# Score runs that wait for their banks' readers, with the rest of each run at the highest priority

## The chip, the core and the metric

The kernel runs on one core of a Trainium2 chip, in one launch. The metric is the device time in microseconds of one execution. The engines named below are TensorE (PE; its weight loads are shown as PEld), VectorE (DVE), ScalarE (ACT), GpSimd (POOL) and SyncE (SP), which issues nearly all DMAs.

## What is computed

One layer of a hybrid backbone for 128 context tokens and 512 latent tokens (a grid of 8 x 64), with width 1024. The core of the reference:

```python
def _trunk_layer(x, mod, ...):
    shift, scale, gate = jnp.split(mod, 3, axis=-1)
    h = _rmsnorm(x, g_pre) * (1 + scale) + shift
    proj = h @ w_in
    qa, ka, va, ga, qr, zf, zb, ir, gr, uf, gf = _split_columns(proj)
    ...
    oa = _context_attention(qa, ka, va)            # context tokens
    oa = _neighbourhood_attention(qa, ka, va, ctx_kv[0], ctx_kv[1], rpb)   # latent tokens
    o_r, s_fin = _hgrn_bidir(qr, zf, zb, ir, lb_f, lb_b, s0)
    o_f = _fourier(uf, w_fnet)
    mixed = jnp.concatenate([oa * silu(ga), o_r * silu(gr), o_f * silu(gf)], axis=-1)
    out = mixed @ w_out
    x = x + gate * _rmsnorm(out, g_post)
```

The attention has 8 heads of 64. A latent token reads keys of its neighbourhood and 256 cached context keys in one softmax; a context token reads the 128 context keys.

## The kernel before

All 640 tokens are normalised, modulated and kept transposed as `hT`, split in a high and a low part so that three products of the short float format make one precise product. Each block of 128 columns of the input projection is 2 x 24 products of 128x320 (`block`), from a weight load `raw` that ACT and DVE split in `hi` and `lo`. Blocks feed the three branches: attention in four pairs of heads (`attention_blocks`, `attention`), the recurrence in two (`recurrence`), the Fourier mixing (`fourier_blocks`, `fourier`), and the gates. At the end `out_first` and `out_second` make the output projection.

The order in which the program is written comes from `Order`: generators run as streams by estimated times. That order gives every instruction its priority; a scheduler, which simulates the engines, then picks on each engine the ready instruction that stands first. So the order on PE is the scheduler's. Afterwards each engine runs its own list strictly in that order, and semaphores hold an instruction until what it needs is done.

A pair of heads in `attention(p)` has five units: `softmax_latent(0..3)`, each for 128 latent tokens, then `softmax_context` (written as unit 4). A latent unit's scores are two calls of `scores`, six products each, which alternate between the two heads (`hh` 1 and 0): head 1 lies in partitions 64 to 127, head 0 in 0 to 63, so that neighbours use different halves of the array. Each head's products go to a bank of its own. `follow` ties each product behind the one before it on PE, but lets others come between. The softmax is a maximum (L675), the addition of the bias table with a maximum (L676), a negation (L678), two exponentials (L679, L680), a sum, a reciprocal and a scaling (L681 to L683) per head. Then `transposes` makes four 128x128 transposes per head into one bank (L124), and `split` brings them out: a cast on ACT (L127) and a subtraction on DVE (L128), two of each. A unit's transposes are written after the scores of the unit behind it (`AHEAD = 2`). `weighted` multiplies with the values.

The banks: eight, of which five rotate for most tiles (`pb` tag "b", the scores and transposes among them) and three for the blocks of the input projection and some others (tag "f"). A tile that gets a bank again waits for the last readers of that bank. There are two buffers `pe` for the exponentials, one for each head.

`mod_cols` makes the modulation: eight products (two instructions each) with 32 columns, on four column strips, for a weight tile.

Of the kernel before, what the change touches and what calls it, by code (L numbers as in the profile page):

```python
# [9 lines left out]
F32 = mybir.dt.float32  # L10
F32R = mybir.dt.float32r
U32 = mybir.dt.uint32
ACT = mybir.ActivationFunctionType
# [4 lines left out]
P = 128  # L18
# [53 lines left out]
def mixer_kernel(ctx: ExitStack, tc: tile.TileContext, A, O):  # L72
    nc = tc.nc
    sc, ve, gp, te, sy = nc.scalar, nc.vector, nc.gpsimd, nc.tensor, nc.sync
# [35 lines left out]
    def mm(out, lhsT, rhs, start=True, stop=True):  # L110
        n, m = rhs.free_size(), lhsT.free_size()
        od.now += 1e-3 * (n * 0.4167 * 4 if rhs.dtype == F32 else max(n * 0.4167, m * 0.83)) + 2e-3
        return te.matmul(out, lhsT, rhs, start=start, stop=stop).ins  # L113

    def follow(chain, ins):

        if chain:
            tc.add_manual_dep(ins, chain[-1].name, mybir.DependencyInfo(mybir.DependencyClass.NoSync,
                                                                        mybir.DependencyReason.DATA), reason="turns")
        chain.append(ins)  # L120
# [4 lines left out]

    def split(src, hi, lo, hi_eng=None, lo_eng=None):
        (sc.copy if hi_eng is None else hi_eng.tensor_copy)(hi, src)  # L127
        (ve if lo_eng is None else lo_eng).tensor_sub(lo, src, hi.bitcast(F32))  # L128


    ident = cp.tile([P, P], F32, tag="ident", name="ident")
# [2 lines left out]
    def const(name, shape, dt=F32, dma=gp.dma_start):  # L134
        t = cp.tile([P, *shape], dt, tag=name, name=name)
        if name in A:
            dma(t, A[name])
        return t
# [6 lines left out]
    RS = [slice(0, 64), slice(64, 128)]  # L145
# [20 lines left out]
    csil = const("csil", [KT, 32])  # L166
# [22 lines left out]
        with tc.issue_after(wdma[-1]) if wdma else ExitStack():  # L189
            sy.dma_start(t, src)  # L190

    def mod_cols(out, w):

        t = od.now
        for k in range(KT):
            o = out[32 * (k % 4):32 * (k % 4) + 32, :]
            mm(o, csil[:, k, :], w[:, k, :], start=(k < 4), stop=(k >= 4))
        od.now = t + 0.45

    shift, G, rstd = const("shift", [KT, 2]), const("G", [KT, 2]), const("rstd", [5])  # L200
# [14 lines left out]
    def load_x():  # L215
        for i in range(5):
            load(xa[i], A["x"][i * P:(i + 1) * P, 0:NT])
            load(xb[i], A["x"][i * P:(i + 1) * P, NT:D])
# [23 lines left out]
    def start_stream():  # L242
        load_x()
        raws, zraw = [], []

        def loads(k):
            for u in range(2):
                raws.append(load_raw(A["wss"][2 * k + u], RAW[2 * k + u]))
            if k < 2:
                zraw.append(load_raw(A["win"][k], "raw"))  # L250

        for k in range(EARLY):
            loads(k)
        scale_x()
        od.now = 11.0
        for k in range(KT):
            if k + EARLY < KT:
                loads(k + EARLY)
            row = sp.tile([P, 256], F32, tag="AC", name=nm("row"), bufs=2)
            pm = PB()  # L260
            for u in range(2):
                mod_cols(pm[:, u * P:(u + 1) * P], raws[2 * k + u])
            yield 0
            ve.tensor_copy(row, pm[:, 0:256])
            yield LAT["row"]

            for u in range(2):
                tr(pm[:, u * P:(u + 1) * P], row[:, u * P:(u + 1) * P])
            pt = S(4)
            ve.reduce_sum(pt, pm[:, 0:256].rearrange("p (u g r) -> p u r g", u=2, r=32)[:, :, 0:2, :], axis=AX.X)  # L270
            ve.tensor_scalar(G[:, k, :], pt[:, 0:2], bss[:, k, 0:1], 1.0, op0=ALU.add, op1=ALU.add)
            ve.tensor_scalar_mul(G[:, k, :], G[:, k, :], gpre[:, k:k + 1])  # L272
            ve.tensor_scalar_add(shift[:, k, :], pt[:, 2:4], bss[:, k, 1:2])
            modulated(k, pm)
            if k < 2:
                zf_w.append(split_w(zraw[k]))
            if k == 1:
                od.set("zw", 0.0)
            yield max(0.0, 13.5 + 2.7 * (k + 1) - od.now)
# [134 lines left out]
    def recurrence(p):  # L414
# [16 lines left out]
        def level(KB, QB, li):  # L431


            mk = late["masks"][:, li, :].unsqueeze(1)
            for i0, i1 in ((0, 4), (4, 5)):
                pa = [PB(), PB()]
                t, chain = od.now, []
                for i in range(i0, i1):
                    for hh in (1, 0):
                        ins = mm(pa[hh][:, (i - i0) * P:(i - i0 + 1) * P], KB[RS[hh], i * P:(i + 1) * P],  # L440
                                 QB[RS[hh], i * P:(i + 1) * P])
                        follow(chain, ins)
                od.now = 0.5 * (t + od.now)
                for hh in range(2):
                    out = AL[:, hh] if i0 == 0 else AC[:, hh:hh + 1, :]
                    src = pa[hh][:, :(i1 - i0) * P].rearrange("p (a t) -> p a t", t=P)
                    if li == 0:
                        sc.copy(out, src)
                    else:
                        ve.copy_predicated(out, mk.to_broadcast([P, i1 - i0, P]), src)  # L450

        for li, h in enumerate(LEVELS):
            QB, KB = T(), T()
# [76 lines left out]
        for i in range(5):  # L530
            o = po[i // 4][:, i % 4 * P:i % 4 * P + P]
# [5 lines left out]
        os_, sq, ss = T(), T(), S(10)  # L537
# [31 lines left out]


    att = [None] * 4

    def attention_blocks(p):
        tbl = sp.tile([P, 2, 2, 256], F32, tag="tbl", name=nm("tbl"), bufs=WB["tbl"])
# [62 lines left out]
    def attention(p):  # L637
        yield f"a{p}"
        tbl, qs, ks, kcs, vs = att[p]

        def scores(outs, qt, keys, chain):

            cols, t = slice(qt * P, (qt + 1) * P), od.now
            for n, (a, b) in enumerate(((0, 0), (0, 1), (1, 0))):
                for hh in (1, 0):
                    follow(chain, mm(outs[hh], qs[a][RS[hh], cols], keys(b)[RS[hh]], start=(n == 0), stop=(n == 2)))
            od.now = 0.5 * (t + od.now)

        os_ = tp.tile([P, NT], F32, tag="o", name=nm("o"), bufs=WB["o"])

        def softmax_context():
            pss, pes = [PB(), PB()], []
            scores([t[:, 0:P] for t in pss], 0, lambda b: ks[b][:, 0:P], [])
            for hh in range(2):
                m, pe = S(4), PE_()
                ve.reduce_max(m[:, 0:1], pss[hh][:, 0:P], axis=AX.X)
                ve.tensor_scalar_mul(m[:, 1:2], m[:, 0:1], -1.0)
                sc.activation(pe[:, 0:P], pss[hh][:, 0:P], ACT.Exp, bias=m[:, 1:2], accum_out=m[:, 2:3])
                ve.reciprocal(m[:, 2:3], m[:, 2:3])
                NE.tensor_scalar(pe[:, :P], pe[:, :P], m[:, 2:3], 0.5, op0=ALU.mult, op1=ALU.mult)  # L660
                pes.append(pe)
            return pes
# [5 lines left out]

        def softmax_latent(qt):
            pss, pes, chain = [PB(), PB()], [], []  # L670
            scores([t[:, 256:512] for t in pss], 1 + qt, lambda b: kcs[b], chain)
            scores([t[:, 0:256] for t in pss], 1 + qt, lambda b: latent_keys(b, qt), chain)
            for hh in range(2):
                m, pe, sb, ss = S(4), PE_(), S(256), pss[hh]
                ve.reduce_max(m[:, 0:1], ss[:, 256:512], axis=AX.X)  # L675
                ve.tensor_tensor_reduce(sb, ss[:, 0:256], tbl[:, int(qt == 3), hh, :], 1.0, m[:, 0:1],  # L676
                                        op0=ALU.add, op1=ALU.max, accum_out=m[:, 1:2])
                ve.tensor_scalar_mul(m[:, 1:2], m[:, 1:2], -1.0)  # L678
                sc.activation(pe[:, 256:512], ss[:, 256:512], ACT.Exp, bias=m[:, 1:2], accum_out=m[:, 3:4])  # L679
                sc.activation(pe[:, 0:256], sb, ACT.Exp, bias=m[:, 1:2], accum_out=m[:, 2:3])  # L680
                ve.tensor_add(m[:, 2:3], m[:, 2:3], m[:, 3:4])  # L681
                ve.reciprocal(m[:, 2:3], m[:, 2:3])
                NE.tensor_scalar(pe, pe, m[:, 2:3], 0.5, op0=ALU.mult, op1=ALU.mult)  # L683
                pes.append(pe)
            return pes
# [19 lines left out]
        def transposes(qt, pe, pT):  # L705
            ptr = PB()
            for g in range(4):

                gd = 1 - g if (qt == 1 and g < 2) else g
                tr(ptr[:, gd * P:(gd + 1) * P], pe[:, g * P:(g + 1) * P])  # L710
            for b in range(2):
                split(ptr[:, b * 256:b * 256 + 256].rearrange("p (g t) -> p g t", t=P),
                      pT[b][0][:, :, qt, :], pT[b][1][:, :, qt, :])

        def weighted(hh, pT):
            r, o = RS[hh], RS[1 - hh]
# [127 lines left out]
    def gate_vectors():  # L844
        selr = cp.tile([P, 2, P], F32R, tag="selr", name="selr")
        gp.tensor_copy(selr, sel)
        for q in range(8):
            yield f"block{WG + q}"
            hf = q // 4
            w = load_raw(A["wg"][q], "raw")  # L850
# [10 lines left out]
            if q % 2 == 0:  # L861
                rows = [sp.tile([P, 256], F32R, tag="AC", name=nm("row"), bufs=2) for _ in range(2)]
            pm, es = PB("f"), slice(q % 2 * P, q % 2 * P + P)
            mod_cols(pm[:, 0:P], w)
            split(pm[:, 0:P], *[t[:, es] for t in rows])
            if q % 2 == 0:
                continue
# [5 lines left out]
            for d in range(2):  # L873
                g = gg[d][hf][:, cs]
# [254 lines left out]
```

## Time and profile before

| | |
|---|---|
| time, median of 3 runs | 437.03 us (436.5 to 437.03) |
| the profiled execution | 437.11 us, span 435.3 us |
| PE busy | 411.3 us (94%) |
| DVE busy | 303.5 us (70%) |
| ACT busy | 205.8 us (47%) |
| DMA | 47.62 MB, mean 109 GB/s |

The span goes from the first instruction to the last; the time has some 1.8 us around it. A row of a timeline has its start and length in us, the engine, the line of the kernel, the operation, out<-in by the program's names, the shape and the count; in brackets stands the idle time before it and what ended it. Lengths of PE's products are modelled and overlap: the pace is read from one start to the next.

### The profile page before, as it was taken

The numbers are of one execution on the slowest core, as the hardware profiler recorded it, in microseconds if no ns is written. First come the engines' busy times: TensorE is split into PE (matmuls) and PEld (weight loads), VectorE is DVE, ScalarE is ACT, GpSimd is POOL, SyncE is SP. The second block draws the span as 40 slices with busy tenths as digits, with TensorE's granted clock in tenths as the row PEclk, the third lists the DMA queues.
The fourth block names the chain that finished last, engine by engine and source line by source line (L and its number), as shares of the span: only waits on it lengthen the run. The fifth ranks groups of instructions, "written<-read, shape, count | busy, mean of one in ns | idle before, by whom it ended". The sixth has DMA issues, their size and how long they took to land.

```text
span 435.3 us, 8309 instructions
## 1 busy us (share of the span) xinstructions
PE 411.3 (94%) x3176; PEld 372.7 (86%) x3176; DVE 303.5 (70%) x866; ACT 205.8 (47%) x546; POOL 7.4 (2%) x23
## 2 busy tenths in 40 slices
PE   0699999999998999999999999999999999999994
PEld 0488899999988998999899889889898988988884
DVE  2775479999986866885597658885768928670174
ACT  6434467565341526654444444753556643350161
POOL 2000000000020100000000000000000000000000
PEclk9999999999999999999999999999999999999998
DMA  7996153211302021122021413245134302481023
GB/s 236 412 407 229 49 158 114 74 45 50 88 20 76 10 62 48 56 97 74 32 68 60 145 50 104 98 147 163 51 119 150 96 0 66 140 291 48 0 105 139
DMA packets 19528, 47.62 MB, mean 109 GB/s; under 512 B 3184, under 2 KB 6912, under 8 KB 19488
## 3 DMA queue, kind: packets, MB, share of 16 engines
q1 hardware_dynamic: 19376, 46.94, 32.0%
q8 instruction: 25, 0.41, 0.4%
q0 software_dynamic: 112, 0.14, 0.3%
q14 instruction: 15, 0.12, 0.1%
HBM read 43.80 MB, written 3.28 MB: 108 GB/s over the span
## 4 chain that ended last, share of the span: by engine, by line
PE 90%; DVE 3%; DMA 3%; ACT 1%; issue 1%; SPq 0%; DVEq 0%; ACTq 0%
PE pb L113 84%; PE pb L124 7%; DMA vs<-wss 2%; DMA txa<-x 1%; DVE AL L450 1%; DVE t L524 1%; DVE AL L487 0%; ACT L679 0%; DVE t L951 0%; ACT pe L680 0%; DVE t L467 0%; DVE t L466 0%; DVE AC L450 0%; DVE t L468 0%; SPq L190 0%
## 5 line engine op out<-in xcount | busy, mean ns | idle before, releaser
L113 PE MATMUL pb<-hT,hi 128*128 128x320 f32 x896 | 208.7, 317 | 2.5 <-DVE vs L128 1.5
L113 PEld LDWEIGHTS pb<-hT,hi 128*128 128x128 f32 x896 | 148.7, 188 | 9.0 <-issue 3.3
L113 PE MATMUL pb<-hT,lo 128*128 128x320 f32 x448 | 139.1, 312 | 0.0
L113 PEld LDWEIGHTS pb<-hT,lo 128*128 128x128 f32 x448 | 84.0, 188 | 1.3 <-DVE G L272 0.2
L128 DVE TENSOR_TENSOR lo<-raw,hi 128x1024 fp32r<-128x1024 f32 x35 | 42.8, 1223 | 18.7 <-ACT hi L127 18.5
L127 ACT CAST hi<-raw 128x1024 fp32r<-128x1024 f32 x35 | 36.8, 1050 | 28.4 <-PE pb L113 17.5
L113 PE MATMUL pb<-t,t 64*128 64x128 f32 (+2 forms) x414 | 42.9, 291 | 0.4 <-DVE AL L450 0.4
L113 PEld LDWEIGHTS pb<-t,t 64*128 64x128 f32 (+1 forms) x414 | 36.0, 188 | 4.7 <-issue 0.7
L127 ACT CAST pT<-pb 128x256 fp32r<-128x256 f32 x64 | 23.5, 373 | 22.3 <-DVE pT L128 11.1
L113 PE MATMUL pb<-hi,mh 128*128 128x512 f32 (+1 forms) x108 | 30.8, 375 | 0.0
L128 DVE TENSOR_TENSOR pT<-pb,pT 128x256 fp32r<-128x256 f32 x64 | 26.5, 419 | 1.7 <-ACT pT L127 1.5
L679 ACT ACTIVATE pe<-pb,s 128x256 f32<-128x256 f32 x32 | 15.3, 478 | 17.5 <-DVE s L678 8.4
L113 PEld LDWEIGHTS pb<-hi,mh 128*128 128x128 f32 x108 | 19.6, 188 | 3.7 <-DVE mh L128 0.3
L113 PE MATMUL pb<-pT,mh 128*128 128x512 f32 (+1 forms) x102 | 21.9, 364 | 0.0
L124 PE MATMUL pb<-ident,pe 128*128 128x128 f32 x136 | 21.0, 274 | 0.5 <-ACT pe L680 0.5
L113 PEld LDWEIGHTS pb<-pT,mh 128*128 128x128 f32 x102 | 17.7, 189 | 3.1
L113 PE MATMUL pb<-lo,mh 128*128 128x512 f32 (+1 forms) x54 | 19.5, 375 | 0.0
L934 ACT ACTIVATE t<-pb 128x512 f32<-128x512 f32 (+1 forms) x11 | 6.1, 552 | 26.9 <-PE pb L113 26.7
L690 DVE TENSOR_TENSOR o<-pb,o 64x512 f32<-64x512 f32 (+1 forms) x16 | 7.8, 486 | 15.5 <-ACT o L689 15.4
L124 PEld LDWEIGHTS pb<-ident,pe 128*128 128x128 f32 x136 | 16.5, 140 | 1.7 <-ACT pe L680 0.7
L450 DVE COPY_PREDICATED AL<-masks,pb 128x512 f32<-128x512 uint32 x24 | 16.6, 742 | 1.7 <-PE pb L113 1.6
L113 PE MATMUL pb<-pT,vs 128*128 128x256 f32 (+1 forms) x96 | 17.0, 320 | 0.0
(205 smaller groups left out, 635.3 us busy)
## 6 DMA issues: line engine op xcount, KB each, us to landing
raw<-win SPq DMA_DIRECT2D x30, 512.0 KB, 3.5
pT<-wss SPq DMA_DIRECT2D x12, 512.0 KB, 10.3
raw<-wg SPq DMA_DIRECT2D x8, 512.0 KB, 3.6
raw<-wout SPq DMA_DIRECT2D x8, 512.0 KB, 3.6
t<-x SPq DMA_DIRECT2D x10, 256.0 KB, 5.4
o_y<-t SPq DMA_DIRECT2D x9, 256.0 KB, 2.2
vs<-wss SPq DMA_DIRECT2D x4, 512.0 KB, 9.5
tbl<-tbl SPq DMA_DIRECT2D x4, 512.0 KB, 3.5
```

What stands on the lines that cost most here:

```text
L113: return te.matmul(out, lhsT, rhs, start=start, stop=stop).ins
L124: last_tr[0] = te.transpose(out, src, ident).ins
L127: (sc.copy if hi_eng is None else hi_eng.tensor_copy)(hi, src)
L128: (ve if lo_eng is None else lo_eng).tensor_sub(lo, src, hi.bitcast(F32))
L450: ve.copy_predicated(out, mk.to_broadcast([P, i1 - i0, P]), src)
L524: ve.scalar_tensor_tensor(sall[r, cdst], sall[r, cs], Td[r, ip:ip + 1], pst[r, cdst], op0=ALU.mult, op1=ALU.add)
L679: sc.activation(pe[:, 256:512], ss[:, 256:512], ACT.Exp, bias=m[:, 1:2], accum_out=m[:, 3:4])
L690: ve.tensor_add(out, src[r, :], out)
L934: sc.activation(T(512)[:, cs], po[:, 0:cs.stop - cs.start], ACT.Square, accum_out=ssb[:, j:j + 1])
```

## The change

`follow` becomes `run_mm`: it issues the product itself, and every product of a chain but the first gets the scheduler's highest priority; the first product can be given instructions that it has to wait for (`after`). The chain's ties stay. The score runs are given as `after` the exponentials L679 (context units: L658) of the unit two before it, counted over all pairs (`readers[-2]`), and the last subtraction of the last split traced (`last_split`). The recurrence's runs and `mod_cols` use `run_mm` without `after`. `split` returns its subtraction.

```diff
-    def follow(chain, ins):
-
+    def run_mm(chain, *args, after=(), **kw):
+        with tc.high_priority() if chain else ExitStack():
+            ins = mm(*args, **kw)
+        for a in () if chain else after:
+            tc.add_manual_dep(ins, a.name, mybir.DependencyInfo(mybir.DependencyClass.Sync, mybir.DependencyReason.DATA),
+                              reason="banks")
         if chain:
             tc.add_manual_dep(ins, chain[-1].name, ...NoSync..., reason="turns")
         chain.append(ins)
...
-    def mod_cols(out, w):
+    def mod_cols(out, w, chain):
         for k in range(KT):
-            mm(o, csil[:, k, :], w[:, k, :], start=(k < 4), stop=(k >= 4))
+            run_mm(chain, out[32 * (k % 4):32 * (k % 4) + 32, :], csil[:, k, :], w[:, k, :], start=(k < 4), stop=(k >= 4))
...
+    last_split = [None]
+    readers = [[], []]
...
-        def scores(outs, qt, keys, chain):
+        def scores(outs, qt, keys, chain, after=()):
-                    follow(chain, mm(outs[hh], qs[a][RS[hh], cols], keys(b)[RS[hh]], start=(n == 0), stop=(n == 2)))
+                    run_mm(chain, outs[hh], qs[a][RS[hh], cols], keys(b)[RS[hh]], start=(n == 0), stop=(n == 2), after=after)
...
         def softmax_latent(qt):
-            scores([t[:, 256:512] for t in pss], 1 + qt, lambda b: kcs[b], chain)
+            scores([t[:, 256:512] for t in pss], 1 + qt, lambda b: kcs[b], chain, readers[-2] + [a for a in last_split if a])
+            readers.append([])
...
-                sc.activation(pe[:, 256:512], ss[:, 256:512], ACT.Exp, bias=m[:, 1:2], accum_out=m[:, 3:4])
+                readers[-1].append(sc.activation(pe[:, 256:512], ss[:, 256:512], ACT.Exp, bias=m[:, 1:2],
+                                                 accum_out=m[:, 3:4]).ins)
...
-                split(ptr[:, b * 256:b * 256 + 256].rearrange("p (g t) -> p g t", t=P),
+                last_split[0] = split(ptr[:, b * 256:b * 256 + 256].rearrange("p (g t) -> p g t", t=P),
```

`softmax_context` is changed like `softmax_latent`. In the lists that follow `pb_2112<-kc_1425,tqs_1421` is a product with the cached keys `kc` and the scaled queries `tqs` into the bank `pb_2112`; `tks` are the latent keys, `pe` the exponentials, and products with `hT` belong to blocks of the input projection. The lines have moved by six to ten.

PE in the first head pair, at the third latent unit (banks 2112 and 2111), before:

```order
L124 MATMUL pb_2102<-ident,pe_1986 128x128 x4
L113 MATMUL pb_2112<-kc_1425,tqs_1421 128x256
L113 MATMUL pb_2305<-hT_106,hi_2301 128x320
L113 MATMUL pb_2305<-hT_105,lo_2302 128x320
L113 MATMUL pb_2305<-hT_105,hi_2301 128x320
L113 MATMUL pb_2305<-hT_106,hi_2301 128x320
L113 MATMUL pb_2305<-hT_105,lo_2302 128x320
L113 MATMUL pb_2111<-kc_1425,tqs_1421 128x256
L113 MATMUL pb_2112<-kc_1426,tqs_1421 128x256
L113 MATMUL pb_2111<-kc_1426,tqs_1421 128x256
```

And after:

```order
L113 MATMUL pb_2112<-kc_1425,tqs_1421 128x256
L113 MATMUL pb_2111<-kc_1425,tqs_1421 128x256
L113 MATMUL pb_2112<-kc_1426,tqs_1421 128x256
L113 MATMUL pb_2111<-kc_1426,tqs_1421 128x256
L113 MATMUL pb_2112<-kc_1425,tqs_1422 128x256
L113 MATMUL pb_2111<-kc_1425,tqs_1422 128x256
L113 MATMUL pb_2112<-tks_1423,tqs_1421 128x256
L113 MATMUL pb_2111<-tks_1423,tqs_1421 128x256
L113 MATMUL pb_2112<-tks_1424,tqs_1421 128x256
L113 MATMUL pb_2111<-tks_1424,tqs_1421 128x256
L113 MATMUL pb_2112<-tks_1423,tqs_1422 128x256
L113 MATMUL pb_2111<-tks_1423,tqs_1422 128x256
```

The run's first product stood alone, five products of a block came before the other eleven; now the twelve stand together, some 6 us of PE work later.

PE in the fourth pair, from the transposes of the third latent unit's second head (`pe_4048`) to the context unit (banks 4161 and 4160), before:

```order
L124 MATMUL pb_4151<-ident,pe_4048 128x128 x4
L113 MATMUL pb_4161<-tks_3550,tqs_3548 128x128
L113 MATMUL pb_4408<-hT_105,hi_4368 128x320
L113 MATMUL pb_4408<-hT_106,hi_4368 128x320
L113 MATMUL pb_4408<-hT_105,lo_4369 128x320
L113 MATMUL pb_4408<-hT_105,hi_4368 128x320
```

And after, from the end of the fourth latent unit's run:

```order
L113 MATMUL pb_4077<-tks_3550,tqs_3549 128x256
L113 MATMUL pb_4076<-tks_3550,tqs_3549 128x256
L130 MATMUL pb_4142<-ident,pe_4037 128x128 x4
L130 MATMUL pb_4151<-ident,pe_4048 128x128 x4
L113 MATMUL pb_4161<-tks_3550,tqs_3548 128x128
L113 MATMUL pb_4160<-tks_3550,tqs_3548 128x128
L113 MATMUL pb_4161<-tks_3551,tqs_3548 128x128
L113 MATMUL pb_4160<-tks_3551,tqs_3548 128x128
L113 MATMUL pb_4161<-tks_3550,tqs_3549 128x128
L113 MATMUL pb_4160<-tks_3550,tqs_3549 128x128
L130 MATMUL pb_4182<-ident,pe_4091 128x128 x4
L130 MATMUL pb_4191<-ident,pe_4102 128x128 x4
```

The products of the block `pb_4408`, which stood between a unit's transposes and the next scores, are gone from here; they now stand ahead of the third latent unit.

DVE in the same place after the change, from the negation of the fourth latent unit's first head to the subtraction that the context run waits for (the last row):

```order
L687 TENSOR_SCALAR s_4090<-s_4090 128x1
L134 TENSOR_TENSOR pT_3997<-pb_4142,pT_3996 128x2x128
L687 TENSOR_SCALAR s_4101<-s_4101 128x1
L691 TENSOR_TENSOR s_4090<-s_4090 128x1
L692 RECIPROCAL s_4090<-s_4090 128x1
L134 TENSOR_TENSOR pT_4010<-pb_4151,pT_4009 128x2x128
L693 TENSOR_SCALAR pe_4091<-pe_4091,s_4090 128x512
L134 TENSOR_TENSOR pT_3999<-pb_4142,pT_3998 128x2x128
L691 TENSOR_TENSOR s_4101<-s_4101 128x1
L692 RECIPROCAL s_4101<-s_4101 128x1
L134 TENSOR_TENSOR pT_4012<-pb_4151,pT_4011 128x2x128
```

The last subtraction of a unit's split stands behind the softmax of the unit that follows.

More of the change, by code (lines that the diff above doesn't have):

```diff
@@ L127, in split @@
         (sc.copy if hi_eng is None else hi_eng.tensor_copy)(hi, src)
-        (ve if lo_eng is None else lo_eng).tensor_sub(lo, src, hi.bitcast(F32))
+        return (ve if lo_eng is None else lo_eng).tensor_sub(lo, src, hi.bitcast(F32)).ins
     ident = cp.tile([P, P], F32, tag="ident", name="ident")
@@ L190, in load @@
             sy.dma_start(t, src)
-    def mod_cols(out, w):
+    def mod_cols(out, w, chain):
         t = od.now
         for k in range(KT):
-            o = out[32 * (k % 4):32 * (k % 4) + 32, :]
-            mm(o, csil[:, k, :], w[:, k, :], start=(k < 4), stop=(k >= 4))
+            run_mm(chain, out[32 * (k % 4):32 * (k % 4) + 32, :], csil[:, k, :], w[:, k, :], start=(k < 4), stop=(k >= 4))
         od.now = t + 0.45
@@ L261, in start_stream @@
             for u in range(2):
-                mod_cols(pm[:, u * P:(u + 1) * P], raws[2 * k + u])
+                mod_cols(pm[:, u * P:(u + 1) * P], raws[2 * k + u], [])
             yield 0
@@ L439, in level @@
                     for hh in (1, 0):
-                        ins = mm(pa[hh][:, (i - i0) * P:(i - i0 + 1) * P], KB[RS[hh], i * P:(i + 1) * P],
-                                 QB[RS[hh], i * P:(i + 1) * P])
-                        follow(chain, ins)
+                        run_mm(chain, pa[hh][:, (i - i0) * P:(i - i0 + 1) * P], KB[RS[hh], i * P:(i + 1) * P],
+                               QB[RS[hh], i * P:(i + 1) * P])
                 od.now = 0.5 * (t + od.now)
@@ L652, in softmax_context @@
             pss, pes = [PB(), PB()], []
-            scores([t[:, 0:P] for t in pss], 0, lambda b: ks[b][:, 0:P], [])
+            scores([t[:, 0:P] for t in pss], 0, lambda b: ks[b][:, 0:P], [], readers[-2] + [a for a in last_split if a])
+            readers.append([])
             for hh in range(2):
@@ L657, in softmax_context @@
                 ve.tensor_scalar_mul(m[:, 1:2], m[:, 0:1], -1.0)
-                sc.activation(pe[:, 0:P], pss[hh][:, 0:P], ACT.Exp, bias=m[:, 1:2], accum_out=m[:, 2:3])
+                readers[-1].append(sc.activation(pe[:, 0:P], pss[hh][:, 0:P], ACT.Exp, bias=m[:, 1:2],
+                                                 accum_out=m[:, 2:3]).ins)
                 ve.reciprocal(m[:, 2:3], m[:, 2:3])
@@ L670, in softmax_latent @@
             pss, pes, chain = [PB(), PB()], [], []
-            scores([t[:, 256:512] for t in pss], 1 + qt, lambda b: kcs[b], chain)
+            scores([t[:, 256:512] for t in pss], 1 + qt, lambda b: kcs[b], chain, readers[-2] + [a for a in last_split if a])
+            readers.append([])
             scores([t[:, 0:256] for t in pss], 1 + qt, lambda b: latent_keys(b, qt), chain)
@@ L711, in transposes @@
             for b in range(2):
-                split(ptr[:, b * 256:b * 256 + 256].rearrange("p (g t) -> p g t", t=P),
-                      pT[b][0][:, :, qt, :], pT[b][1][:, :, qt, :])
+                last_split[0] = split(ptr[:, b * 256:b * 256 + 256].rearrange("p (g t) -> p g t", t=P),
+                                      pT[b][0][:, :, qt, :], pT[b][1][:, :, qt, :])
         def weighted(hh, pT):
@@ L863, in gate_vectors @@
             pm, es = PB("f"), slice(q % 2 * P, q % 2 * P + P)
-            mod_cols(pm[:, 0:P], w)
+            mod_cols(pm[:, 0:P], w, [])
             split(pm[:, 0:P], *[t[:, es] for t in rows])
```

## The prediction

> **What bounds the kernel now.** I read the page's busy times first, then the chain that ended last, then what TensorE waited for. The first two lines give the span and each engine's busy time and instructions; the third the shares of the last chain; the rest who PE waited for, with the us, the times and the longest.
>
> ```profile
> span 435.3 us, 8309 instructions
> PE 411.3 (94%) x3176; PEld 372.7 (86%) x3176; DVE 303.5 (70%) x866; ACT 205.8 (47%) x546; POOL 7.4 (2%) x23
> PE 90%; DVE 3%; DMA 3%; ACT 1%; issue 1%; SPq 0%; DVEq 0%; ACTq 0%
> ...
> PE pb L113 <- DMA vs<-wss: 14.5, 1, 14.5
> PE pb L113 <- DVE vs L128: 1.5, 1, 1.5
> PE pb L113 <- ACT t L324: 1.0, 1, 1.0
> PE pb L124 <- ACT pe L680: 0.5, 1, 0.5
> PE pb L113 <- DVE AL L450: 0.4, 1, 0.4
> ```
>
> After the first 14.5 us, which is the load of the first weights, TensorE (PE) waits for 3.4 us in the whole program, and 90% of the chain that ended last is PE. So the time is PE's issue time plus its waits, and any new wait of PE lengthens the program one for one. There is almost nothing left to remove on the side of waits: a gain has to come from cheaper issue. The change can give that, because score products (64 of the array's 128 rows each) are cheap side by side and dear alone. Below, from the timeline (start us, length us, engine, line, operation, count), are one run that stands whole, and one cut after its first product.
>
> ```profile
> 225.24 0.62 PE L113 MATMUL pb<-kc,tqs 64*128 64x256 f32 x6
> 225.69 0.51 PE L113 MATMUL pb<-tks,tqs 64*128 64x256 f32 x6
> 226.14 0.41 PE L113 MATMUL pb<-hT,lo 128*128 128x320 f32 x1
> ...
> 177.15 0.38 PE L113 MATMUL pb<-kc,tqs 64*128 64x256 f32 x1
> 177.46 0.41 PE L113 MATMUL pb<-hT,hi 128*128 128x320 f32 x1
> ...
> 178.38 0.61 PE L113 MATMUL pb<-kc,tqs 64*128 64x256 f32 x5
> 178.72 0.62 PE L113 MATMUL pb<-tks,tqs 64*128 64x256 f32 x6
> 179.27 0.56 PE L113 MATMUL pb<-hT,hi 128*128 128x320 f32 x2
> ```
>
> The whole run holds PE from 225.24 to 226.14: 0.90 us. The cut one holds it 0.31 us for the first product (177.15 to 177.46) and 0.89 us for the other eleven (178.38 to 179.27), and each entry into the 64-row form costs about 0.09 us more than the usual step. A cut costs 0.31 + 0.09 = 0.40 us.
>
> **The change part by part. First, the high priority of a run's further products.** By the order of the two programs the 20 score runs stand in 36 pieces before and in 27 after: nine cuts go, 9 x 0.40 = 3.6 us less PE time. Six runs remain cut after the first product (the first has no high priority, and in those the second bank comes free later). The modulation products (32 columns each, eight to a call) now get the same priority: 25 pieces become 19.
>
> ```profile
> 318.45 0.65 PE L113 MATMUL pb<-raw,csil 128*32 128x128 f32 x16
> ...
> 329.17 0.41 PE L113 MATMUL pb<-raw,csil 128*32 128x128 f32 x2
> 330.10 0.64 PE L113 MATMUL pb<-raw,csil 128*32 128x128 f32 x14
> ```
>
> Sixteen instructions cost 0.65 us in one piece and 0.41 + 0.64 in two; the ends overlap with what follows, so I price a cut at 0.2 us, half of the difference (bounds 0.1 and 0.4): 6 x 0.2 = 1.2 us less. On the other side the first two runs of the first head pair now alternate product by product, so that in eight places two products of the same half follow each other and can't share the array; at 0.1 us each (a third of the lone product's 0.31) that is 0.8 us more. The recurrence's runs stand in 17 pieces before and after: nothing. Issue time in sum: -3.6 - 1.2 + 0.8 = -4.0 us. Bounds: -2.5 and -5.5.
>
> **Second, the wait of a run's first product.** It waits for the exponentials of the unit two before and for the last split of the transposes traced last. PE issues in order, so everything behind it waits too. In the first three head pairs the order leaves room. The slowest path from a score run to the next run's permission is leg 2 below, 6.6 us; the context run follows the last latent run by 8.0, 8.8 and 6.4 us of PE work (counted in products at the prices above) in pairs 0, 1 and 2. Only pair 2 is short, by 0.2 us. Pair 3 is different: its units have slipped by some 10 us against the weight blocks, which are not held, and the blocks that filled PE's time between its units now stand ahead of them. From the third latent run to the last transposes PE has just eight other products, where before some 15 us of other products stood between them. Four places lose there. The rows are those of the same operations before.
>
> ```profile
> 340.77 0.46 PE L113 MATMUL pb<-hT,hi 128*128 128x320 f32 x2
> 341.06 0.31 PE L113 MATMUL pb<-hT,lo 128*128 128x320 f32 x1
> 341.21 1.89 PE L113 MATMUL pb<-t,cs 128*128 128x256 f32 x8
> 341.26 1.04 ACT L127 CAST hi<-raw 128x1024 fp32r<-128x1024 f32 x1 [0.17 <-PE pb L113]
> 342.34 1.23 DVE L128 TENSOR_TENSOR lo<-raw,hi 128x1024 fp32r<-128x1024 f32 x1 [0.39 <-ACT hi L127]
> 343.48 0.48 DVE L128 TENSOR_TENSOR t<-pb,t 128x320 fp32r<-128x320 f32 x1
> ```
>
> Leg 0: the block behind the Fourier input needs the bank that this last 128x320 subtraction frees. It ends at 343.96, 2.9 us after the block's last product at 341.06, and PE can go on at about 3.0. Before, a context run and eight transposes stood there; after, only the two small products' 1.6 us: 1.4 us lost.
>
> ```profile
> 329.51 0.66 PE L124 MATMUL pb<-ident,pe 128*128 128x128 f32 x4
> ...
> 333.06 0.42 DVE L128 TENSOR_TENSOR pT<-pb,pT 128x256 fp32r<-128x256 f32 x1
> ...
> 355.36 2.21 PE L113 MATMUL pb<-t,t 128*128 128x512 f32 x9
> ```
>
> Leg 1: from a unit's last transposes (329.51) to the end of their last split (333.48) took 4.0 us, since the vector engine puts the next softmax between. After, PE has until the fourth latent run the transposes (0.45), four 128x512 products (4 x 0.23) and four 128x320 products (4 x 0.145): 1.95 us. The run waits the other 2.1 us.
>
> ```profile
> 333.27 0.62 PE L113 MATMUL pb<-kc,tqs 64*128 64x256 f32 x5
> 334.29 0.76 DVE L675 TENSOR_REDUCE s<-pb 128x1 f32<-128x256 f32 x2 [0.41 <-PE pb L113]
> 336.24 0.48 DVE L676 CUSTOM_DVE_ANT_0 m<-pb,tbl,s 128x256 f32<-128x256 f32 x1
> 336.64 0.48 DVE L676 CUSTOM_DVE_ANT_0 m<-pb,tbl,s 128x256 f32<-128x256 f32 x1
> 336.64 0.37 ACT L127 CAST pT<-pb 128x256 fp32r<-128x256 f32 x1
> 338.83 0.48 ACT L679 ACTIVATE pe<-pb,s 128x256 f32<-128x256 f32 x1
> ...
> 341.14 0.41 DVE L128 TENSOR_TENSOR pT<-pb,pT 128x256 fp32r<-128x256 f32 x1
> ```
>
> Leg 2, from the fourth latent run to the context run: the run until the maxima can start (1.1, a product more than 333.27 to 334.29), two maxima 0.76, two bias additions 0.88, a negation and a split between 0.5 (a split is the row at 341.14), then from the first exponential to the end of the last split 2.7 (338.83 to 341.55) and two more casts that now stand between the exponentials, 2 x 0.35: 6.6 us. PE has the run itself and eight transposes, 1.85 us: 4.8 us lost. Leg 3: behind the last transposes the weighted sum waits for one cast and the Fourier products for one copy, after 1.8 us of PE work; by casts of 0.37 us that queue in a row I take 0.6 us (bounds 0 and 2). The scalar and vector engines are not behind in this sum: they are what PE waits for, and after the softmax of the last unit the wait moves on to the split after it.
>
> Sum: -4.0 + 0.2 + 1.4 + 2.1 + 4.8 + 0.6 = +5.1 us. The bounds of the legs together: 4.5 us, if the splits overtake the softmax on the vector engine, and 12 us, if loads of weights fall late as well; so +0.5 to +8 with the issue bounds left at the middle.
>
> **What else moves.** On SP's queue three loads of bias tables go one or two places behind weight loads. A table is read at the earliest when the next pair's first run is done, more than 10 us of PE work later by the new order, so I cost it at nothing; without that cover it would be one landing.
>
> ```profile
> tbl<-tbl SPq DMA_DIRECT2D x4, 512.0 KB, 3.5
> ```
>
> Behind pair 3 the Fourier stage and the output projection stand in the same order; there PE alone sets the pace, so what was lost isn't made up.
>
> **The time.** The profiled execution took 437.11 us for its span of 435.3, close to the median of 437.03. 437.0 + 5.1 = 442.1; I say 442.0.
>
> **Rivals.** (a) *The waits stay hidden and the issue gain is left*: 437.0 - 4.0 = 433 us. For it: PE waited only 3.4 us before, so the order was good at hiding such chains. It decides if legs 0 to 3 together cost under 3.1 us instead of 8.9. Against it: the path of leg 2 has no other PE work beside it. Chance 0.15. (b) *Gain and waits cancel*, legs of 3 to 5 us, within 0.2% (0.9 us, about what a measurement of this kernel can tell from no change): 436.2 to 437.9. Chance 0.09. (c) *The array runs slower after the long gap.* The first modulation products, after 14.5 us of idle, took longer than the same sixteen later:
>
> ```profile
> 14.54 1.08 PE L113 MATMUL pb<-vs,csil 128*32 128x128 f32 x16 [14.54 <-DMA vs<-wss]
> ...
> 18.63 1.08 PE L113 MATMUL pb<-pT,csil 128*32 128x128 f32 x16
> ...
> 14.00:16.00 2.00, 1.46 (x18) 1.11 (x19) 1.96 (x8) 0.29 (x1) 0.00 (x0) 1.00 1.04 418
> ```
>
> 1.08 against 0.65 us, still so at 18.63, 4 us on, while the granted clock's column says 1.00. If the 4.8 us gap of leg 2 brought that back for 5 us, it would cost 5 x (1 - 0.65/1.08) = 2.0 us: 444 us. Nothing before shows a gap of that length between busy stretches, so I give it 0.14. [...] (d) *Faster issue doesn't come about*: if a cut cost only its 0.31 us and the modulation pieces nothing, the issue gain would be 2.0 us and the time 444; it has no chance of its own and is in the range.
>
> **Chances.** My forecast (legs above the gain, 438 to 445 us) 0.62, (c) 0.14, (a) 0.15, (b) 0.09. Slower by over 0.2% therefore 0.76, within it 0.09, faster 0.15. The range goes from 435.5, which leaves out most of (a), to 445.5: two in ten stay outside. The forecast's own range is 439.5 to 444.5.
>
> **What would show it.** Score runs after the change of 0.90 us in one piece, about nine lone products fewer. In the waits of PE, three or four new ones of 1 to 5 us on the split (`DVE pT`) or a scale or exponential of `pe`, all in one stretch of 15 to 20 us near 340 us of the span, and PE ahead of the old trace by 3 to 4 us until then. It would be wrong if PE entered that stretch with more than eight other products to issue, or if waits as long came up in the first three pairs.

## The result: slower by 0.7%, and the profile after

The changed kernel took 439.78 us (median of 3, 439.76 to 440.7) against 437.03 before: ratio 1.0073, 95% interval 1.0058 to 1.0088. The profiled execution took 440.7 us for a span of 438.9, 3.6 us more than the span of before. First the page's header lines, the shares of the last chain, and PE's waits (us in all, times, longest) of the kernel after.

```profile
span 438.9 us, 8301 instructions
PE 407.1 (93%) x3176; PEld 371.6 (85%) x3176; DVE 305.6 (70%) x866; ACT 204.3 (47%) x546; POOL 7.4 (2%) x23
PE 82%; DVE 8%; DMA 5%; ACT 3%; issue 1%; SPq 0%; DVEq 0%; ACTq 0%
...
PE pb L113 <- DMA vs<-wss: 14.2, 1, 14.2
PE pb L113 <- DVE pT L134: 5.8, 2, 4.3
PE pb L113 <- DVE vs L134: 1.5, 1, 1.5
PE pb L113 <- ACT t L329: 1.0, 1, 1.0
PE pb L113 <- DVE t L134: 0.9, 1, 0.9
PE pb L113 <- DVE row L134: 0.9, 1, 0.9
```

PE is 4.2 us less busy, so issue did get cheaper. But 7.6 us of new waits stand in the list: 5.8 on the split of the transposes (`pT`), 0.9 on the subtraction of the block's split (`t`), 0.9 on a split `row` of the gate vectors. PE's share of the last chain fell from 90% to 82%, DVE's rose from 3% to 8%. PE's timeline shows the places. In the fences with dots, rows in between are left out.

```profile
326.20 0.60 PE L130 MATMUL pb<-ident,pe 128*128 128x128 f32 x4
327.73 0.62 PE L113 MATMUL pb<-row,selr 128*128 128x256 f32 x3 [0.94 <-DVE row L134]
...
331.71 1.89 PE L113 MATMUL pb<-t,cs 128*128 128x256 f32 x8
334.54 0.56 PE L113 MATMUL pb<-hT,hi 128*128 128x320 f32 x2 [0.95 <-DVE t L134]
...
337.67 0.63 PE L113 MATMUL pb<-kc,tqs 64*128 64x256 f32 x6
338.13 0.52 PE L113 MATMUL pb<-tks,tqs 64*128 64x256 f32 x6
338.58 1.09 PE L130 MATMUL pb<-ident,pe 128*128 128x128 f32 x8
339.43 1.17 PE L113 MATMUL pb<-t,t 128*128 128x512 f32 x4
...
342.72 0.62 PE L113 MATMUL pb<-kc,tqs 64*128 64x256 f32 x6 [1.53 <-DVE pT L134]
...
343.63 1.22 PE L130 MATMUL pb<-ident,pe 128*128 128x128 f32 x8
349.11 0.55 PE L113 MATMUL pb<-tks,tqs 64*128 64x128 f32 x6 [4.26 <-DVE pT L134]
349.59 1.85 PE L130 MATMUL pb<-ident,pe 128*128 128x128 f32 x8
351.09 3.06 PE L113 MATMUL pb<-t,t 128*128 128x512 f32 x8
```

A whole score run now holds PE from 337.67 to 338.58, 0.91 us in one piece. Counted from one start to the next against the usual step, the waits lost 1.18 us (at 327.73), 1.34 (334.54), 1.60 (342.72) and 4.33 (349.11). The last one ends with DVE's last split of the transposes, here the first and the last such row behind the fourth latent run (342.72):

```profile
344.32 0.37 ACT L133 CAST pT<-pb 128x256 fp32r<-128x256 f32 x1 [1.16 <-PE pb L130]
...
348.55 0.41 DVE L134 TENSOR_TENSOR pT<-pb,pT 128x256 fp32r<-128x256 f32 x1
```

It ends at 348.96, and the context run starts at 349.11. Behind that gap comes a loss that is no wait: eight transposes take 1.85 us instead of 1.09, eight products of 128x512 take 3.06 us. The windows (stretch, its length, PE busy with its instructions, granted clock, DMA share, GB/s) say why. First two of before, in which PE is busy throughout at a clock of 1.00, then those of after:

```profile
346.00:348.00 2.00, 2.00 (x16) 1.00 0.26 96
350.00:352.00 2.00, 2.00 (x12) 1.00 0.00 0
```

```profile
346.00:348.00 2.00, 0.00 (x0) 1.00 0.00 0
348.00:350.00 2.00, 0.89 (x9) 0.94 0.00 0
350.00:352.00 2.00, 2.00 (x9) 0.50 0.03 8
352.00:354.00 2.00, 2.00 (x8) 0.71 0.00 0
354.00:356.00 2.00, 2.00 (x10) 1.00 0.00 0
```

The granted clock was 0.50 for 0.24 + 2.00 + 1.16 = 3.4 us; in windows of 0.1 us it is 1.00 up to 349.7 and 0.50 from 349.8 to 353.1. PE was busy in all of it, so by my estimate that cost some 1.7 us. Before, the column says 1.00 from 322 to 358 us, and PE was busy in all of it.

### The profile page after: what moved, and what is told of

Its sections match the earlier page's. It is cut to its first block, busy times and chain, and to the rows that moved or that the text cites. A ratio compares the mean times of both kernels' runs of the same rounds, so it can differ in the third digit from the quotient of the medians.

```text
span 438.9 us, 8301 instructions
## 1 busy us (share of the span) xinstructions
PE 407.1 (93%) x3176; PEld 371.6 (85%) x3176; DVE 305.6 (70%) x866; ACT 204.3 (47%) x546; POOL 7.4 (2%) x23
## 4 chain that ended last, share of the span: by engine, by line
PE 82%; DVE 8%; DMA 5%; ACT 3%; issue 1%; SPq 0%; DVEq 0%; ACTq 0%
PE pb L113 76%; PE pb L130 6%; DMA raw<-win 2%; DMA vs<-wss 1%; DMA txa<-x 1%; ACT pe L690 1%; ACT pe L688 1%; DVE lo L134 1%; DVE m L685 1%; DVE s L684 1%; DVE AL L454 1%; DVE t L528 1%; ACT hi L133 0%; DVE pe L693 0%; DVE pT L134 0%
## 5 line engine op out<-in xcount | busy, mean ns | idle before, releaser
L133 ACT CAST hi<-raw 128x1024 fp32r<-128x1024 f32 x35 | 36.8, 1050 | 40.7 <-PE pb L113 22.8
L113 PE MATMUL pb<-t,t 64*128 64x128 f32 (+2 forms) x414 | 44.4, 294 | 0.4 <-DVE AL L454 0.4
L113 PEld LDWEIGHTS pb<-t,t 64*128 64x128 f32 (+1 forms) x414 | 36.9, 190 | 4.9 <-issue 0.7
L113 PE MATMUL pb<-hi,mh 128*128 128x512 f32 (+1 forms) x108 | 32.1, 376 | 0.0
L684 DVE TENSOR_REDUCE s<-pb 128x1 f32<-128x256 f32 x32 | 11.9, 417 | 7.7 <-PE pb L113 7.7
## 6 DMA issues: line engine op xcount, KB each, us to landing
pT<-wss SPq DMA_DIRECT2D x12, 512.0 KB, 10.2
```

## Experiments: what each half of the change does

The twelve kernels were each timed against the kernel before on the same chip (436.4 to 436.6 us there). "Pieces" counts the stretches of PE's list into which the 20 score runs and the modulation calls are cut: 36 and 25 before, 27 and 19 after. My theory A: the added wait makes the runs whole and also makes the stalls, because the fourth pair's units have no other PE work beside them; the priority mends the modulation calls. Its rivals stand with each run.

**Priority alone.** All `after` arguments are taken away:

```diff
-            scores(..., chain, readers[-2] + [a for a in last_split if a])
+            scores(..., chain)
```

> The high priority alone: no run of scores waits for readers. Theory A (the wait keeps the runs whole and at the same time makes the stalls of pair 3; the priority alone mends only the modulation's pieces): 37 pieces of score runs stand in this order and 19 of modulation products (36 and 25 before), so 6 x 0.2 = 1.2 us is gained and 0.4 lost: 435.5 to 437 us, and no wait of PE over 2 us after the first load. Rival B (the priority brings the gain of some 6 us, the waits only cost): 430 to 433 us.

435.2 us, ratio 0.9968 (0.9957 to 0.998); 37 score pieces, 19 modulation pieces. Theory A; rival B falls. Priority does not keep a run together. The reason that I see in the order is that the second product's bank isn't free yet, and a priority can't help an instruction that isn't ready. The 1.2 us gained are the modulation calls', in spite of one more score cut.

**Waits alone.** `run_mm` keeps `after`, the priority goes:

```diff
-        with tc.high_priority() if chain else ExitStack():
+        with ExitStack():
```

> The waits alone, no high priority. Theory A: 28 pieces of score runs and 23 of modulation products stand in this order, so most of the gain in issue is there (8 x 0.40 + 2 x 0.2 = 3.6 us or more), and so is the stall behind the third unit's transposes in pair 3, 4 to 5 us, with smaller ones beside it: 437 to 441 us. Rival B: without the priority the runs cost what they cost before, and the stalls come on top: 443 to 446 us.

438.47 us, ratio 1.0044 (1.003 to 1.0058); 28 and 23 pieces, 4.0 us of waits on `pT`, the longest 3.1. So the waits alone make the runs whole, and the stalls with them. Theory A; rival B falls.

**Which of the two waits.** The exponentials are left out of `after`, the last split stays:

```diff
-            scores(..., chain, readers[-2] + [a for a in last_split if a])
+            scores(..., chain, [a for a in last_split if a])
```

> As after the change, but no score run waits for the exponentials of the unit two before; the wait for the last split stays. The lists of all five engines are those of after the change, row by row. Theory A (the last split comes after those exponentials anyway, so the second half of the wait decides everything): the same waits, 1.2, 1.3, 1.6 and 4.3 us near 325 to 350 us, and 438 to 440.5 us. Rival D (the exponentials' waits hold PE now and then): waits shorter by 1 us or more in sum and 435 to 437.5 us.

440.17 us, ratio 1.008 (1.0066 to 1.0093), and the same list on every engine as after the change. Its waits:

```profile
PE pb L113 <- DVE pT L134: 5.8, 2, 4.3
PE pb L113 <- DVE t L134: 0.9, 1, 0.9
```

So the wait for the exponentials, half of what the change says of itself, decides nothing: the last split comes later anyway. (Conversely, with the exponentials alone all engines' lists are those of priority alone, row by row; that version wasn't run.) Theory A, but for the wait on `row`, which I had expected again and which was absent in this execution.

**Modulation calls without the priority.** In `mod_cols`, `run_mm` becomes `mm` again:

```diff
-            run_mm(chain, out[...], csil[:, k, :], w[:, k, :], start=(k < 4), stop=(k >= 4))
+            mm(out[...], csil[:, k, :], w[:, k, :], start=(k < 4), stop=(k >= 4))
```

> As after the change, but the modulation products have the ordinary priority: 24 modulation pieces instead of 19, score runs and waits as after (the waits of 1.3, 1.6 and 4.3 us stay). Theory A (a modulation cut costs about 0.2 us): 0.5 to 1.5 us over the kernel after, 440.2 to 441.5 us, if that stands at 439.8 on this chip. Rival G (a modulation cut costs nothing): within 0.4 us of the kernel after, 439.4 to 440.2 us.

441.9 us, ratio 1.0117 (1.01 to 1.0135); 24 modulation and 26 score pieces. Compared by ratio with the split-wait version, which has the changed kernel's lists, that is 0.0037, or 1.6 us for five cuts: some 0.3 us a cut. Theory A by its kind, a little over its upper end. The price is rough: this version has one score cut less (26 pieces for 27), and the clock was low for longer in the profiled execution, 10.2 us against 6.8 (last section).

## Experiments: where the stall comes from

**The context unit without its wait.** In the fourth pair the context run no longer waits for the last split:

```diff
-            scores(..., [], readers[-2] + [a for a in last_split if a])
+            scores(..., [], readers[-2] + ([a for a in last_split if a] if p < 3 else []))
```

> As after the change, but the context unit of the fourth pair no longer waits for the last split (all other waits stay; the order keeps 27 score pieces and 19 modulation pieces). Theory A (the 4.3 us belong to a chain scores, softmax, split, transposes that has nothing beside it; without the wait the context products go at once and their transposes wait instead, as in the run without waits in the fourth pair): the wait of 4.3 us goes, the first two waits of 1.3 and 1.6 us stay, and two waits of 1 to 2 us come on an exponential or scale of the context unit, so 437.5 to 439.5 us, still slower than the kernel before by 0.2 to 0.7%. Rival B (the added wait itself is the stall, and what is behind it is hidden): 433 to 436 us.

438.38 us, ratio 1.0041 (1.0026 to 1.0056). The longest wait goes, and two others take its place:

```profile
346.18 0.55 PE L113 MATMUL pb<-tks,tqs 64*128 64x128 f32 x5 [1.22 <-ACT pe L688]
347.98 3.40 PE L113 MATMUL pb<-t,t 128*128 128x512 f32 x8 [1.26 <-DVE t L805]
```

The chain scores, softmax, split, transposes is still alone on the machine; PE only meets it two steps later. Rival B falls.

**No waits in the fourth pair.** As above for all five units (`... if p < 3 else ()`).

> As the changed kernel, but in the fourth pair of heads no run waits for readers. Theory A (the loss is the waits of pair 3 alone, 9 us in one stretch): by the order the issue time is about as in the changed kernel (29 pieces), the block's products stand between the units of pair 3 again, and the stalls of 1.3, 1.6 and 4.3 us are gone: 430 to 434 us. Rival C (pair 3 is late whatever its runs wait for, since pairs 0 to 2 are late, and PE has nothing else to do then): a stall of 4 us or more stays, 437 to 440 us.

436.54 us, ratio 1.0004 (0.999 to 1.0018): both expectations missed. The waits of the change are gone, yet PE still runs dry, with 29 score pieces:

```profile
343.23 0.55 PE L113 MATMUL pb<-tks,tqs 64*128 64x128 f32 x5 [1.58 <-ACT pe L688]
345.04 3.21 PE L113 MATMUL pb<-t,t 128*128 128x512 f32 x8 [1.26 <-DVE t L805]
```

So theory A had to be widened: the waits of the first three pairs move the fourth pair's units late against the weight blocks, and what then makes PE stall is the lack of other products, with or without a wait there. The next versions ask that. The clock shows here too: of the twelve executions two kept a mean clock of 0.999 and took 435.2 us; the others, at 0.988 to 0.992, took 436.4 to 438.5.

**The gate block ga2 earlier**, to put products into the gap:

```diff
-FILL = "... P3 gf0 gf1 uf0 F0 ga2 ga3"
+FILL = "... P3 gf0 gf1 ga2 uf0 F0 ga3"
```

> As the changed kernel, but the gate block ga2 is written ahead of the first Fourier block, so that its 48 products can stand beside pair 3 without a bank that the Fourier stage holds. Theory A: more products beside the units; leg 1 and the wait for the block's bank (1.3 and 1.6 us) go, the 4.3 us wait shrinks or stays, since no product stands between the third unit's transposes and the context run here either: 433 to 438 us. Rival C: as before, 439 to 441 us.

438.77 us, ratio 1.0047 (1.003 to 1.0064). The two earlier waits went, the one ahead of the context run stayed at 3.1 us, and a new one of 1.8 us on `mh` came 25 us later. A miss, just over its upper end: the block filled the places ahead of the gap and not the gap itself, and was missing later.

**Waits in the first two pairs only** (`... if p < 2 else ()` in both calls):

> As after the change, but only the first two pairs' score runs wait; the last two have priority alone (32 score pieces, 19 modulation pieces). Theory A (the waits gain where blocks stand between the units, that is early, and lose where the units have slipped against the blocks): most of the issue gain of the first pairs without the waits near 340 us, 433 to 435.5 us, faster than the kernel before by 0.2 to 0.8%. Rival C (any wait in the early pairs shifts the later units far enough that PE runs dry near 340 us again): 436.5 to 439 us.

433.3 us, ratio 0.9924 (0.9906 to 0.9943); 32 and 19 pieces, PE's waits are the five that the kernel before has, and the clock is 1.00 near 340 us. Theory A. Against the version without waits in the fourth pair, only the waits of the third pair are gone, and PE no longer runs dry. Whether they would do it without those of the first two is not shown.

**The fourth pair earlier, without waits in it.** The gate block ga2 also moves ahead of the first Fourier block, as above:

```diff
-FILL = "... P2 gr0 gr1 ga1 P3 gf0 gf1 uf0 F0 ga2 ga3"
+FILL = "... P2 gr0 P3 gr1 ga1 gf0 gf1 ga2 uf0 F0 ga3"
```

> As after the change, with the fourth pair handed to the order right behind the gate block gr0 of the recurrence, ahead of gr1, ga1, gf0 and gf1, and without waits in the fourth pair (29 score pieces, 19 modulation pieces). Theory A (the loss is PE having too little other work between the fourth pair's units; with more blocks left for it the issue gain remains): no wait over 1 us near 340 us, granted clock 1.00 there, 432.5 to 435 us. Rival C (the chain of the fourth pair waits wherever it stands): waits of 3 us or more in the fourth pair, 436.5 to 439.5 us.

431.17 us, ratio 0.9874 (0.986 to 0.9889), with 29 and 19 pieces: the fastest of all, and below the range of theory A: I had priced the gain too low. PE in the place that stalled, from the transposes of the third latent unit's second head on:

```profile
span 429.1 us, 8294 instructions
...
341.90 0.60 PE L130 MATMUL pb<-ident,pe 128*128 128x128 f32 x4
342.43 0.32 PE L113 MATMUL pb<-tks,tqs 64*128 64x128 f32 x1
342.69 0.70 PE L113 MATMUL pb<-t,cs 128*128 128x256 f32 x2
343.44 0.55 PE L113 MATMUL pb<-tks,tqs 64*128 64x128 f32 x5
343.92 0.56 PE L113 MATMUL pb<-hT,hi 128*128 128x320 f32 x2
...
348.47 0.60 PE L130 MATMUL pb<-ident,pe 128*128 128x128 f32 x4
```

Between the context run (to 343.92) and the transposes of the fourth latent unit's first head (348.47) now stand 4.5 us of block and Fourier products, in place of the gaps.

**Three controls for that version**: its new order (the fourth pair's place and ga2's) in the kernel before, with priority alone, and with the whole change.

> The kernel before (no wait, no added priority), with only the fourth pair handed to the order ahead of gr1, ga1, gf0 and gf1, as in the fastest version so far. 36 score pieces and 25 modulation pieces, as before. Theory A (that version's gain is whole runs and whole modulation calls; the place of the fourth pair only keeps PE supplied, which it was already): 435.5 to 438 us, the same as the kernel before. Rival E (the place of the fourth pair alone makes that version's gain): 431 to 433.5 us.

> As the version with priority alone (no waits), with the fourth pair in the earlier place. 36 score pieces, 19 modulation pieces. Theory A (priority alone mends the modulation calls and no score run): 434 to 436 us, as priority alone in the old place, 435.2. Rival E (the place gives the gain): 430.5 to 433 us.

> The whole change, waits in all four pairs, with the fourth pair in the earlier place. 26 score pieces, 19 modulation pieces. Theory A (the context unit of the fourth pair has beside its chain only the last latent run and eight transposes, wherever the pair stands, so its wait stays, and with it the half clock; the other waits go): one PE wait of 3 to 4.5 us on DVE pT, one of 1 to 2 us, granted clock near 0.5 for 3 to 6 us behind, 433.5 to 437 us. Rival F (with blocks left beside the fourth pair no wait is over 1 us): 430 to 432 us, as without waits in that pair.

| fourth pair in the earlier place | pieces | us | ratio (95%) |
|---|---|---|---|
| kernel before | 36, 25 | 437.61 | 1.002 (1.0009 to 1.003) |
| priority alone | 36, 19 | 434.56 | 0.9959 (0.9944 to 0.9974) |
| waits in pairs 0 to 2, priority | 29, 19 | 431.17 | 0.9874 (0.986 to 0.9889) |
| the whole change | 26, 19 | 436.21 | 0.999 (0.9977 to 1.0002) |

The order alone gains nothing, so rival E falls. Priority makes the six modulation calls whole and gains 3.0 us, more than the 1.2 in the old order; of this the profiled executions show 1.9 (spans of 434.7 and 432.8 us). Seven cuts fewer in the score runs gain 3.4 us more, 0.48 a cut; and the waits in the fourth pair, for three cuts fewer, lose 5.0 us. All four have both moves of the order, so what ga2's place does by itself is not shown. The last row's profile has the same stall as the change itself, so rival F falls:

```profile
341.37 0.56 PE L113 MATMUL pb<-hT,hi 128*128 128x320 f32 x2 [1.05 <-DVE t L134]
...
346.69 1.09 PE L130 MATMUL pb<-ident,pe 128*128 128x128 f32 x8
350.82 0.55 PE L113 MATMUL pb<-tks,tqs 64*128 64x128 f32 x6 [3.04 <-DVE pT L134]
```

## Why the prediction was right, and where its sum was not

The direction, the cause and the place were right: slower, by waits of PE on `pT` and on the block's split, all between 326 and 351 us (a stretch of 25 us, where I had said 15 to 20), and none in the first three pairs. The time came out at 439.78 instead of 442.0.

- **Issue, priced at -4.0 us, was about -5.6**, at my bound of -5.5. The waits lost 1.18 + 1.34 + 1.60 + 4.33 + 0.35 = 8.8 us and the clock of 0.50 some 1.7, while the old order had lost about 1 us in the same stretch in small irregular steps between products (counted over the starts of all products in both traces): 9.5 us in all. The span grew by 3.6 us, but the start of the program differs between executions (last section). Counted from the fifth modulation call, which starts at 22.80 us before and 22.50 after, it grew by 3.9, so 5.6 were gained. Likewise the version without stalls (fourth pair earlier), where that call starts at 21.59, is 5.0 us shorter from there on (6.2 by the whole span), with two cuts more than the change. By terms: a score cut, priced 0.40, measured 0.48 (seven cuts, 3.4 us) and 0.38 (five cuts, 1.9 us by ratio between priority alone and the waits in two pairs), so its price held. A modulation cut, priced 0.2, measured about 0.3 (1.2 us from priority alone for six cuts, in spite of a score cut), and up to 0.5 in the new order. And the alternation of the first two runs, +0.8, cost nothing; this is the term that was wrong in kind. Their 24 products stand in three pieces before and after, of 0.98, 0.51 and 0.74 us in both traces, though after the change neighbours use the same half in eight places. Here are the last eight products before and after; after the change four of their neighbours share a half:

```profile
164.91 0.74 PE L113 MATMUL pb<-tks,tqs 64*128 64x256 f32 x8
```

```profile
164.16 0.74 PE L113 MATMUL pb<-tks,tqs 64*128 64x256 f32 x8
```

I had priced a half behind the same half from a product that stood alone, 0.31 us, which is another thing: inside these pieces the products start in pairs, 1 to 10 ns apart, and past the first pair the next one starts 0.11 to 0.12 us later, before and after. By the measured prices the sum is 9 x 0.43 + 6 x 0.3 = 5.7 us.

- **Legs 0, 1 and 2, priced at 1.4, 2.1 and 4.8 us, measured 1.34, 1.60 and 4.33.** The path of leg 2, 6.6 us by its rows of before, took 342.72 to 349.11, 6.4 us. Reading a future chain from the durations of the same operations in the old trace worked to within 0.5 us. Leg 3, 0.6 us, shows at most as one step that is 0.35 us too long, at 351.09, inside the half clock: 7.6 us in all for 8.9. Pair 2's shortfall of 0.2 us did not show as a wait.
- **A leg that I had not seen**: 1.18 us on the split `row` at 327.73, ahead of leg 0. It came again with the context unit freed (1.2 us), but not in the split-wait version, whose lists are the same as after the change; it isn't a fixed part.
- **Rival (c) came true, on top and not instead.** The granted clock was 0.50 for 3.4 us behind the longest gap, 4.26 us, which cost some 1.7 us; I had said 5 us and 2.0, with a chance of 0.14. The case for it was better than that: the first products of the program had shown slow rows, 1.08 us against 0.65, behind an idle stretch of 14.5 us, and a gap of 4.8 us was my own forecast. The forecast and the rival were not exclusive, and should have been one case.
- **The step not asked**: whether both halves of the wait matter. The exponentials decide nothing, the last split everything; the legs were computed from the split alone, so the sum didn't suffer.

So the losses, put at 9.1 us with pair 2, came to 9.5, made up otherwise than I said: shorter legs, and the `row` wait and the slow clock in their place. That the two sums agree is luck. For the profiled execution the account closes: +5.1 forecast, 1.6 less for issue, 0.4 more for the losses, 0.3 less for the start of the program, +3.6 measured. The rest of the 2.2 us between 442.0 and the median of 439.78 is that the profiled execution, 440.7, was the longest of the three. Without the half clock the profiled execution would have stood at 440.7 - 1.7 = 439.0 us, still slower than before.

## What to carry over

An instruction that waited held everything behind it on its engine's list (PE started nothing in the 4.26 us ahead of the context run), so a wait that keeps a group together is worth adding only where other work of that engine stands between the group and the end of the wait: here it gained about 0.4 us a cut in the first pairs and lost 5 us in the last. A higher priority can't keep a group together whose members become ready at different times; it helped only the calls whose operands were all there. And when a change leaves PE idle, price the slow clock behind it as part of the same case: here one gap of 4.26 us, and in another version two of 1.58 and 1.26 us close together, each stood ahead of 3.4 us at a clock of 0.50.

## What the runs showed of the hardware

In eight of the profiled executions the granted clock fell to 0.50 between 344 and 353 us. Worked out from the windows, the low stretches last 3.4 us (after the change, in the two versions whose context unit is freed, and with the whole change in the earlier place), 6.8 us (waits alone, ga2 earlier, split wait alone) or 10.2 us (plain modulation calls): once, twice and three times the same length. The split-wait version has the changed kernel's lists and the same gap of 4.26 us, and yet its clock fell inside the gap and stayed low for 1.20 + 4.00 + 1.64 = 6.8 us:

```profile
344.00:346.00 2.00, 0.00 (x0) 0.70 0.00 0
346.00:348.00 2.00, 0.91 (x7) 0.50 0.00 0
348.00:350.00 2.00, 2.00 (x9) 0.50 0.03 8
350.00:352.00 2.00, 2.00 (x7) 0.59 0.00 0
```

So the same gap had 3.4 us at the low clock with it in one execution and 6.8 us in the other, and the six executions of the split-wait version took from 439.04 to 440.47 us. The clock also fell where PE was not idle throughout: with no waits in the fourth pair the two gaps were 1.58 and 1.26 us with five score products between them.

```profile
342.00:344.00 2.00, 0.55 (x5) 1.00 0.00 0
344.00:346.00 2.00, 0.96 (x4) 0.94 0.00 0
346.00:348.00 2.00, 2.00 (x6) 0.50 0.00 0
348.00:350.00 2.00, 2.00 (x12) 0.71 0.00 0
```

The 3.4 us ahead of the fall (at 345.8) held some 1.3 us of PE work. The two short waits had as long a low stretch behind them, 0.24 + 2.00 + 1.16 = 3.4 us, as the gap of 4.26 us after the change. In all eight traces the 3.4 us ahead of the fall held 0.6 to 1.9 us of PE work. A border can't be read from this. After the change the stretches of 3.4 us from 339.5 and from 342.9 held 1.87 and 1.95 us of PE work, PE did nothing at all from 345 to 349, and the clock was 1.00 in all of that and fell at 349.8; with plain modulation calls the 3.4 us ahead of the fall held 1.9 us. On the way back, the clock rose behind 3.4 us at 0.50 with 3.2 us of work in them (the whole change in the earlier place), and stayed low behind 3.4 us with 3.1 (waits alone) or 3.0 (ga2 earlier), two of the longer stretches.

The pace at the start of the program differs between executions too. In the fastest version (fourth pair earlier) the modulation call at 17.51 us is already fast:

```profile
15.51 1.08 PE L113 MATMUL pb<-pT,csil 128*32 128x128 f32 x16
17.51 0.65 PE L113 MATMUL pb<-pT,csil 128*32 128x128 f32 x16
```

After the change such a call still takes 1.08 us at 20.54, and 0.65 only at 22.50. The early start is in part eaten by a wait of 1.4 us on `hT`, which the changed kernel's trace does not have. The clock's column says 1.00 from 14 to 24 us after the change, so it does not show this part. With a first load that lands between 13.7 and 14.5 us, this puts the fifth modulation call anywhere from 21.6 to 22.8 us, so a difference of 1.2 us between two profiled spans need not come from the change.
